# Encoder step on one core: the output product keeps six of its eight weight blocks between its last two column chunks, and the feed-forward layer's first operands are made while those chunks run

## The chip, the cores and the metric

The kernel runs on one core of a Trainium2 chip. The metric is the device time of one execution in microseconds (us); lower is better. Runs of the kernel before took 2792.56, 2794.83 and 2790.57 us (median 2792.56).

## The reference

One step of a two-layer encoder over 1024 prompt frames and 64 sample frames (1088 columns, 1024 features). Each layer adds a mixer (attention in layer 0; forgetting attention and a recurrent branch in layer 1) and a SwiGLU feed-forward network (FFN) to `x`, each behind an RMS norm. The change touches the end of the mixer, where its outputs are multiplied by `w_out` and added to `x`, and the start of the FFN:

```
o_a = (rmsnorm(o_a, a_subln_g) * (1.0 - lam_init)).reshape(nb, T, A_WIDTH)
o_b = o_b.reshape(nb, T, B_WIDTH)
return jnp.concatenate([o_a, o_b], axis=-1) @ w_out, new_state
...
yp = yp + mp
yp = yp + swiglu(rmsnorm(yp, norm_ffn_g[layer]), ffn_w1[layer], ffn_w3[layer], ffn_w2[layer])
...
def swiglu(h, w1, w3, w2):
    return (jax.nn.silu(h @ w1) * (h @ w3)) @ w2
```

The 64 sample frames go through the same products with the same weights.

## The kernel before

Every fp32 operand of a large product is cut into a high and a low part: `split` (L216) copies the high part on ScalarE (ACT, L217) and subtracts it from the operand on VectorE (DVE) or GpSimd (POOL, L218) for the low part. A product is then three matmuls on TensorE (PE): high·high, high·low, low·high. Features lie on 128 partitions in eight blocks; the 1088 columns are cut into three chunks of 384, 384 and 320.

**The output product.** `wout` (L822) runs chunk 0, then 1, then 2. In each chunk it takes the eight weight blocks of 128 output features two at a time, in the order 0, 2, 4, 6. `loadw` (L220) loads a block of 512 KB (128x1024) into one of two raw slots, `split` makes its high part on ACT and its low part on POOL, and these go into one of four slots that a ring hands out (`w_o`). So all eight blocks are loaded and split anew in every chunk: 24 loads a layer. After the last matmuls of a pair (L246 in `gemm_steps`), L848 on DVE adds the product in the PSUM banks to `x`, and `addsq` (L266) squares the result on ACT (L271 for a chunk's first block, L274 for the others) and adds it to the chunk's sum on DVE (L275). When a chunk's eight blocks are done, `rms` (L250) sums over partitions with a matmul of ones (L256), forms the inverse root by Ln (L260, L262) and Exp (L263) on ACT, and `norm_x` (L888) scales the eight blocks of `x` on DVE (L892).

**The first superblock of the FFN.** The two first FFN products are computed in a form with seven products of half-size blocks (`superblock`, L984): its PE instructions are L1000, each 128x272, 168 of them in a superblock. The right-hand operands T0 to T6 are sums and differences of normalised blocks of `x`, in high and low parts; `fill_x` (L899) makes them on ACT and DVE (L217, L218; the differences are L925), once for columns 0 to 543 (`p` = 0), once for columns 544 to 1087 (`p` = 1). The left-hand operands come from two weight blocks: `raws` (L961) loads them into two of three raw slots, and `left` (L940) makes four sums and differences of 128x512 on POOL (L953 to L956), seven high parts on ACT and seven low parts of 128x512 on the engine it is told. For superblock 0, `open_ffn` (L972) calls it ahead of the last pair of chunk 2 and has the low parts made on DVE; later superblocks have them on POOL. Superblock 0 runs `p` = 0 before `p` = 1, the later ones both together. L1004, L1008, L1010 (and L1061, L1062 with Silu) take the results from the banks.

**What sets the order.** The program is written as Python that emits instructions; a scheduler (the Tile framework) then puts them in an order for each engine, and inserts semaphores where data or a slot has to be waited for. Each engine runs its own list strictly in order. All loads and stores are issued by one queue, SP (L170). ACT loads a table of functions where the next function is not in the loaded one (`ACT_TABLE_LOAD`): Ln and Exp share one table, Silu is in another.

Of the kernel before, what the change touches and what calls it, by code (L numbers as in the profile page):

```python
# [58 lines left out]
F_RAW3 = (1024, 2048, 13440)  # L59
F_SUM = (14464, 14976)  # L60
F_C = (11776, 12320, 12864)
F_SG = (9600, 7424, 6144)
HB = 272
# [64 lines left out]
class Kernel:  # L128
    def __init__(self, tc, M, MR, PS, xTd, oTd, ed, fd, hd, I, O):
# [15 lines left out]
        self.w_o = at([0, 1024, R_Q[0], R_Q[0] + 1024]), at([2048, 3072, R_Q[0] + 2048, R_K[0]])  # L145
# [676 lines left out]
    def wout(self, W, gcol, src, l):  # L822
# [13 lines left out]
        def products(ms, ws, ci, ring):  # L836

            c0, n = CH[ci]
            for m in ms:
                self.dma(self.x[m][ci], src[m * 128:m * 128 + 128, c0:c0 + n])  # L840
            ps = [ring.get()[:, :n] for _ in ms]
            for p, w in zip(ps, ws):
                yield from self.gemm_steps(p, w, c0, n, oh, ol, ks[:-1], last=False)
            yield "w", 1
            for m, p, w in zip(ms, ps, ws):
                xs = self.x[m][ci]
                yield from self.gemm_steps(p, w, c0, n, oh, ol, ks[-1:], first=False)
                nc.vector.tensor_tensor(xs, p, xs, op=ALU.add)  # L848
                self.addsq(ci, m, xs)
                self.dma(self.xTd[m * 128:m * 128 + 128, c0:c0 + n], xs)  # L850

        load(0)
# [10 lines left out]
        fill = self.fill_x(0)  # L863
        ws = [self.loadw(W[i], self.w_o) for i in range(2)]
        for m in (0, 2, 4, 6):
            now = ws
            if m < 6:
                ws = [self.loadw(W[m + 2 + i], self.w_o) for i in range(2)]
            else:
                self.open_ffn(l)  # L870
            yield from products((m, m + 1), now, 2, self.mmf)
            if fill and m < 6:
                fill.pop(0)()
        self.tmp = self.tmp3
        r = self.rms(2)
        for f in fill:
            f()
        self.norm_x(2, gcol, r)
        for f in self.fill_x(1):
            f()  # L880
# [18 lines left out]
    def fill_x(self, p):  # L899
# [15 lines left out]
        def pieces(*hs):  # L915
            return [(0, HB)] if all(h == whole for h in hs) else list(zip(cuts, cuts[1:]))

        def put(i, f, h):
            for s, e in pieces(h):
# [3 lines left out]
        def sub(to, a, b):  # L923
            for s, e in pieces(to[1], a[1], b[1]):
# [3 lines left out]
        def mid():  # L928
            sub(b11, b12, b11)
            sub(b12, b22, b12)  # L930
            sub(b22, b22, b11)
            put(3, *b22)

        def end():
            sub(b21, b21, b22)
            put(6, *b21)
        return [lambda: put(0, *b11), lambda: put(1, *b21), lambda: put(2, *b22), mid,
                lambda: put(4, *b11), lambda: put(5, *b12), end]

    def left(self, a, b, adds, subs):  # L940

        a11, a12, a21, a22 = a[:, 0:512], a[:, 512:1024], b[:, 0:512], b[:, 512:1024]
        s1, s2 = (self.v(o, 512) for o in F_SUM)
# [10 lines left out]
        adds.tensor_tensor(s2, s1, a11, op=ALU.subtract)  # L954
        adds.tensor_tensor(a12, a12, s2, op=ALU.subtract)
        adds.tensor_tensor(a21, a11, a21, op=ALU.subtract)  # L956
        yield got
        for x in (a12, s2, s1, a21, a22):
            yield put(x)

    def raws(self, s):  # L961
# [3 lines left out]
        for j in (s - s % 2, s - s % 2 + 1):  # L965
            raw = self.v(F_RAW3[self.ri % 3], 1024)
# [5 lines left out]
    def open_ffn(self, l):  # L972
# [5 lines left out]
        r = self.raws(0)  # L978
        self.ops = list(self.left(*r, self.nc.gpsimd, self.nc.vector))
# [507 lines left out]
```

## Time and profile before

| | value |
|---|---|
| median of three runs | 2792.56 us (2790.57 to 2794.83) |
| the profiled execution: time, span | 2788.72 us, 2786.9 us |
| mean granted TensorE clock | 0.976 of full speed |
| busy share of the span: PE, DVE, ACT, POOL | 94%, 50%, 44%, 46% |
| loads of `w_out` blocks, both layers | 48 of 512 KB |
| layer 0: chunk 1's sum over partitions (L256), end of chunk 2's matmuls, chunk 2's L256, PE without a stop from | 645.04, 674.58, 690.25, 718.76 us |
| layer 1: the same | 1982.31, 2011.13, 2022.90, 2052.68 us |

The times of the last two rows are counted from the start of the span; a row of the timeline gives a start, a duration, the engine, the line, the operation with its operands, a count, and in brackets the idle time before it with what ended it. Neighbouring instructions of one shape are drawn together (x176), short gaps included. In the windows view the columns are the busy time of each engine inside a stretch.

### The profile page before, as it was taken

How to read it: one execution, taken by the hardware profiler on the slowest of the kernel's cores; microseconds unless marked ns; L12 is line 12 of the kernel's file. 1: busy time of each engine (PE TensorE's matmuls, PEld its weight loads, DVE VectorE, ACT ScalarE, POOL GpSimd, SP SyncE). 2: the span in 40 equal slices, each digit the busy share in tenths (PEclk: the TensorE clock that was granted, in tenths of full speed). 3: DMA queues.
4: the chain of work that ended last, by engine and by line, in shares of the span. 5: the costliest groups of instructions: out<-in, count | busy, mean ns of one | idle time of the engine just before them, and what ended most of it. 6: DMA issues, size and time to landing. Idle time of an engine off the chain costs nothing.

```text
span 2786.9 us, 45330 instructions
## 1 busy us (share of the span) xinstructions
PE 2615.1 (94%) x17614; PEld 2539.0 (91%) x17614; DVE 1405.8 (50%) x2753; ACT 1239.3 (44%) x2413; POOL 1284.4 (46%) x996
## 2 busy tenths in 40 slices
PE   6999999987899999999988789998889999999997
PEld 5899999987899999999978789988789999999997
DVE  7666666778532332422267547777962332342225
ACT  5666677754323323311245556676433323331113
POOL 5222222334766766312474333343566666741235
PEclk9999999998999999999999899999999999999998
DMA  6222222353222222532342342245422222244224
GB/s 197 69 70 73 69 62 63 114 170 116 78 102 70 79 78 78 192 102 70 108 139 36 47 88 79 76 124 163 129 83 90 86 78 70 79 157 143 70 65 143
DMA packets 122167, 272.11 MB, mean 98 GB/s; under 512 B 22216, under 2 KB 71632, under 8 KB 121952
## 3 DMA queue, kind: packets, MB, share of 16 engines
q1 hardware_dynamic: 121952, 269.22, 31.7%
q8 instruction: 138, 2.26, 0.3%
q14 instruction: 77, 0.63, 0.1%
HBM read 200.98 MB, written 65.43 MB: 96 GB/s over the span
## 4 chain that ended last, share of the span: by engine, by line
PE 71%; DVE 10%; ACT 6%; DMA 5%; POOL 3%; issue 3%; SPq 0%; DVEq 0%; ACTq 0%; POOLq 0%
PE banks L1000 31%; PE banks L246 13%; PE banks L1101 5%; PE banks L1102 5%; PE banks L1100 5%; DVE split_arena L218 3%; ACT split_arena L217 3%; PE banks L574 3%; POOL split_arena L218 2%; PE banks L457 2%; PE banks L458 1%; PE banks L499 1%; PE banks L500 1%; DVE arena L275 1%; DMA arena<-o_spill 1%
## 5 line engine op out<-in xcount | busy, mean ns | idle before, releaser
L218 POOL TENSOR_TENSOR split_arena<-arena,split_arena 128x512 fp32r<-128x512 f32 (+5 forms) x536 | 852.0, 1596 | 1129.6 <-ACT split_arena L217 1050.4
L217 ACT ACTIVATE split_arena<-arena 128x512 fp32r<-128x512 f32 (+10 forms) x713 | 506.7, 723 | 1130.3 <-PE banks L1000 439.2
L1000 PE MATMUL banks<-split_arena 128*128 128x272 f32 x7392 | 942.3, 290 | 39.8 <-ACT split_arena L217 16.1
L1000 PEld LDWEIGHTS banks<-split_arena 128*128 128x128 f32 x7392 | 937.8, 190 | 44.0 <-ACT split_arena L217 23.2
L246 PE MATMUL banks<-split_arena 128*128 128x384 f32 (+1 forms) x3528 | 666.4, 336 | 18.0 <-DVE arena L1264 7.1
L246 PEld LDWEIGHTS banks<-split_arena 128*128 128x128 f32 x3528 | 590.3, 192 | 28.1 <-DVE arena L1264 7.4
L1100 PE MATMUL banks<-split_arena 128*128 128x384 f32 (+1 forms) x1056 | 347.7, 329 | 4.7 <-DVE arena L1067 2.9
L1102 PE MATMUL banks<-split_arena 128*128 128x384 f32 (+1 forms) x1056 | 347.0, 329 | 2.4 <-POOL split_arena L218 2.4
L1101 PE MATMUL banks<-split_arena 128*128 128x384 f32 (+1 forms) x1056 | 346.4, 328 | 2.3 <-DVE split_arena L218 2.3
L218 DVE TENSOR_TENSOR split_arena<-arena,split_arena 128x1088 fp32r<-128x1088 f32 (+11 forms) x177 | 197.7, 1128 | 75.3 <-ACT split_arena L217 74.2
L218 DVE TENSOR_TENSOR split_arena<-banks,split_arena 128x512 fp32r<-128x512 f32 (+4 forms) x312 | 167.7, 542 | 97.4 <-ACT split_arena L217 94.7
L1100 PEld LDWEIGHTS banks<-split_arena 128*128 128x128 f32 x1056 | 200.0, 189 | 7.2 <-ACT split_arena L217 3.3
L1102 PEld LDWEIGHTS banks<-split_arena 128*128 128x128 f32 x1056 | 199.9, 189 | 3.3 <-POOL split_arena L218 3.1
L1101 PEld LDWEIGHTS banks<-split_arena 128*128 128x128 f32 x1056 | 200.1, 189 | 3.0 <-DVE split_arena L218 2.6
L469 DVE CUSTOM_DVE_ANT_0 arena<-banks,arena 128x384 f32<-128x384 f32 (+4 forms) x368 | 175.6, 494 | 47.1 <-PE banks L458 39.8
L217 ACT ACTIVATE split_arena<-banks 128x512 fp32r<-128x512 f32 (+4 forms) x312 | 146.8, 476 | 110.5 <-PE banks L574 46.1
L1008 DVE TENSOR_TENSOR arena<-banks,arena 128x544 f32<-128x544 f32 (+1 forms) x46 | 32.0, 699 | 295.4 <-PE banks L1000 295.4
L1121 DVE TENSOR_TENSOR arena<-banks,arena 128x384 f32<-128x384 f32 (+1 forms) x96 | 51.4, 535 | 251.7 <-PE banks L1102 251.5
L471 ACT ACTIVATE arena<-arena 128x640 f32<-128x640 f32 (+8 forms) x216 | 156.3, 724 | 42.8 <-DVE arena L469 41.3
L574 PE MATMUL banks<-arena 128*128 128x128 f32 (+2 forms) x828 | 133.3, 273 | 13.4 <-ACT arena L492 6.2
L574 PEld LDWEIGHTS banks<-arena 128*128 128x128 f32 (+2 forms) x828 | 95.4, 140 | 30.4 <-ACT arena L492 11.2
L457 PE MATMUL banks<-split_arena 128*128 128x256 f32 (+3 forms) x312 | 113.1, 364 | 6.4 <-DVE arena L469 4.3
(166 smaller groups left out, 3071.8 us busy)
## 6 DMA issues: line engine op xcount, KB each, us to landing
arena<-in_w_dram SPq DMA_DIRECT2D x120, 512.0 KB, 3.5
h_spill<-arena SPq DMA_DIRECT2D x22, 1088.0 KB, 4.3
arena<-h_spill SPq DMA_DIRECT2D x44, 544.0 KB, 4.7
arena<-in_w_dram SPq DMA_DIRECT2D x48, 384.0 KB, 3.2
arena<-in_abw_dram SPq DMA_DIRECT2D x24, 512.0 KB, 3.6
arena<-in_abo_dram SPq DMA_DIRECT2D x24, 512.0 KB, 3.7
arena<-in_cdo_dram SPq DMA_DIRECT2D x24, 512.0 KB, 3.6
arena<-in_cdw_dram SPq DMA_DIRECT2D x20, 512.0 KB, 3.7
```

Source lines behind the costliest of these rows:

```text
L217: self.nc.scalar.activation(hi, x, AF.Copy)
L218: return sub.tensor_tensor(lo, x, hi.bitcast(F32), op=ALU.subtract)
L246: self.pe = self.nc.tensor.matmul(ps, x[:, k], y[k][:, c0:c0 + n], start=a and i == 0, stop=z and i == 2).ins
L457: nc.tensor.matmul(ps[:, :mw], qd[:, q0:q0 + m], kk[:, k0 + s:k0 + s + mw], start=True, stop=False)
L469: nc.vector.tensor_tensor_reduce(o, p, t, -1.0, low, ALU.add, ALU.min, to)
L471: nc.scalar.activation(sb, sb, AF.Exp, bias=st[:, 0:1], scale=-1.0, accum_out=st[:, 1:2])
L574: nc.tensor.transpose(pt[:r, t * nq + s * m:t * nq + s * m + m], src, self.ident[:m, :m])
L1000: nc.tensor.matmul(bank[:, p], l[:, k], r[:, k, x], start=first and i == 0, stop=k == 3 and i == 2, skip_group_check=True)
L1100: nc.tensor.matmul(ps, wh, h[:, c0:c0 + n], start=j == j0, stop=False)
L1101: nc.tensor.matmul(ps, wh, lo[:, c0:c0 + n], start=False, stop=False)
L1102: nc.tensor.matmul(ps, wl, h[:, c0:c0 + n], start=False, stop=j == j1 - 1)
L1121: nc.vector.tensor_tensor(xs, ps, xs, op=ALU.add)
```

## The change

- The ring of four slots becomes six fixed pairs of slots (a pair holds the high and low parts of two blocks) a, b and c; c lies where the attention kept data that is dead by then. Chunk 0 takes the blocks as before through a and b. Then c is filled with blocks 0 and 1. Chunk 1 runs 6 (in b), 4 (in a), 0 (in c), 2 (loaded into b once 6 is done); chunk 2 runs 4, 0, 2 from the slots where they lie, and 6, loaded into a once 4 is done. A layer has 14 loads and splits of blocks instead of 24. The first block of a chunk, which starts the sum of squares, is now 0, 6 or 4.
- `open_ffn` is called after chunk 2's first pair instead of ahead of its last. There are four raw slots instead of three, the first of which (14464) is not shared with the raw weight slots, so that its load does not wait for them. Three of the steps of `left` are emitted after the pair 0, the others after the pair 2. The seven low parts of superblock 0 are made on POOL instead of DVE, and the sum that had a buffer of its own now takes the place of a block it used.
- `fill_x` is cut into finer steps. For `p` = 0, T0, T1 and parts of two differences come in chunk 1 and T2, T3 in chunk 2 (T2, which lies in c, once that is free); T4 to T6 come after chunk 2. For `p` = 1 only T0 and T1's first part (224 columns) is emitted ahead of chunk 2's end.

```diff
-        self.w_o = at([0, 1024, R_Q[0], R_Q[0] + 1024]), at([2048, 3072, R_Q[0] + 2048, R_K[0]])
+        self.w_o = (0, 1024, R_Q[0], R_Q[0] + 1024, R_Q[1], R_QL[0]), (2048, 3072, R_Q[0] + 2048, R_K[0], R_Q[1] + 1024, R_QL[0] + 1024)
...
-                self.addsq(ci, m, xs)
+                self.addsq(ci, m, xs, first=m == (0, 6, 4)[ci])
...
-        for m in (0, 2, 4, 6):
-            yield from products((m, m + 1), [self.loadw(W[m + i], self.w_o) for i in range(2)], 0, self.mma)
+        a, b, c = (tuple(zip(*(x[i:i + 2] for x in self.w_o))) for i in (0, 2, 4))
+        def weights(m, at):
+            return [self.loadw(W[m + i], [Ring(self.MR, [o], 1024) for o in at[i]]) for i in range(2)]
+        for m, at in ((0, a), (2, b), (4, a), (6, b)):
+            ws[m] = weights(m, at)
+            yield from products((m, m + 1), ws[m], 0, self.mma)
...
+        ws[0] = weights(0, c)
         self.norm_x(0, gcol)
-        for m in (0, 2, 4, 6):
-            yield from products((m, m + 1), [self.loadw(W[m + i], self.w_o) for i in range(2)], 1, self.mmf)
+        one, two = self.fill_x(0), self.fill_x(1)
+        for m in (6, 4, 0, 2):
+            yield from products((m, m + 1), ws[m], 1, self.mmf)
+            if m == 6:
+                ws[2] = weights(2, b)
+            else:
+                one.pop(0)()
         self.norm_x(1, gcol)
...
+        for m in (4, 0, 2, 6):
+            yield from products((m, m + 1), ws[m], 2, self.mmf)
+            if m == 4:
+                ws[6] = weights(6, a)
+                first = self.open_ffn(l)
+                one.pop(0)()
+            elif m == 0:
+                self.ops = [next(first) for _ in range(3)]
+                one.pop(0)()
+                two.pop(0)()
+            elif m == 2:
+                self.ops += list(first)
+                one.pop(0)()
...
-        self.ops = list(self.left(*r, self.nc.gpsimd, self.nc.vector))
+        return self.left(*self.raws(0), self.nc.gpsimd, self.nc.gpsimd)
```

Three places in the engines' own order matter later; all are from layer 0, and lines behind the change have shifted (L892 became L908, L925 L942, L953 to L956 L980 to L983, L1004 L1030, L1062 L1088).

ACT at the end of chunk 2, before: Ln and Exp of chunk 2's norm (L262, L263) stand together, ahead of the first Silu (L1062).

```order
L274 ACTIVATE arena<-arena 128x320 x2
L1004 ACTIVATE arena<-banks 128x272
L262 ACTIVATE arena<-banks,arena 128x320
L263 ACTIVATE arena<-arena 128x320
L1062 ACT_TABLE_LOAD
L1062 ACTIVATE arena<-banks 128x272
```

The same place of ACT after the change.

```order
L274 ACTIVATE arena<-arena 128x320 x2
L1030 ACTIVATE arena<-banks 128x272
L262 ACTIVATE arena<-banks,arena 128x320
L1088 ACT_TABLE_LOAD
L1088 ACTIVATE arena<-banks 128x272
L263 ACT_TABLE_LOAD
L263 ACTIVATE arena<-arena 128x320
```

A table load, the first Silu and a second table load now stand between Ln and Exp. In layer 1 they do not; there the order is as before.

POOL from chunk 0 to the first FFN operands, before: the x22 are the last splits of weight blocks of all three chunks, and the adds of `left` follow.

```order
L218 TENSOR_TENSOR split_arena<-arena,split_arena 128x1024 x22
L953 TENSOR_TENSOR arena<-arena 128x512
L954 TENSOR_TENSOR arena<-arena 128x512
L956 TENSOR_TENSOR arena<-arena 128x512
L955 TENSOR_TENSOR arena<-arena 128x512
```

The same place of POOL after the change; the two 128x512 in the second row are the first low parts of FFN operands, the x2 behind them blocks 6 and 7 for chunk 2.

```order
L218 TENSOR_TENSOR split_arena<-arena,split_arena 128x1024 x10
L218 TENSOR_TENSOR split_arena<-arena,split_arena 128x512 x2
L218 TENSOR_TENSOR split_arena<-arena,split_arena 128x1024 x2
L980 TENSOR_TENSOR arena<-arena 128x512
L981 TENSOR_TENSOR arena<-arena 128x512
L218 TENSOR_TENSOR split_arena<-arena,split_arena 128x512
L982 TENSOR_TENSOR arena<-arena 128x512
L218 TENSOR_TENSOR split_arena<-arena,split_arena 128x512
L983 TENSOR_TENSOR arena<-arena 128x512
L218 TENSOR_TENSOR split_arena<-arena,split_arena 128x512 x5
```

Ten splits of 128x1024 are gone, and superblock 0's low parts stand between and behind its adds; the last three of the x5 include two of superblock 0 and one of superblock 1.

DVE between the second pair of chunk 2 and the last, before: the 128x512 are the seven low parts of superblock 0.

```order
L848 TENSOR_TENSOR arena<-banks,arena 128x320 x2
L925 TENSOR_TENSOR arena<-arena 128x4x160
L275 TENSOR_TENSOR arena<-arena 128x320 x2
L218 TENSOR_TENSOR split_arena<-arena,split_arena 128x512 x2
L848 TENSOR_TENSOR arena<-banks,arena 128x320 x2
L218 TENSOR_TENSOR split_arena<-arena,split_arena 128x4x272
L275 TENSOR_TENSOR arena<-arena 128x320
L218 TENSOR_TENSOR split_arena<-arena,split_arena 128x512
L275 TENSOR_TENSOR arena<-arena 128x320
L218 TENSOR_TENSOR split_arena<-arena,split_arena 128x512 x4
L848 TENSOR_TENSOR arena<-banks,arena 128x320 x2
```

The same stretch of DVE after the change.

```order
L848 TENSOR_TENSOR arena<-banks,arena 128x320 x2
L942 TENSOR_TENSOR arena<-arena 128x4x112
L275 TENSOR_TENSOR arena<-arena 128x320
L942 TENSOR_TENSOR arena<-arena 128x4x160
L275 TENSOR_TENSOR arena<-arena 128x320
L942 TENSOR_TENSOR arena<-arena 128x4x112
L942 TENSOR_TENSOR arena<-arena 128x4x160
L848 TENSOR_TENSOR arena<-banks,arena 128x320 x2
L218 TENSOR_TENSOR split_arena<-arena,split_arena 128x4x112
L275 TENSOR_TENSOR arena<-arena 128x320
L218 TENSOR_TENSOR split_arena<-arena,split_arena 128x4x160
L275 TENSOR_TENSOR arena<-arena 128x320
```

No 128x512 is left, and pieces of the differences and of T3 (112 and 160 columns) stand in their place. On PE, chunk 2's L256 stands behind 28 matmuls of superblock 0 in each layer, where it stood behind 19 in layer 0 and 22 in layer 1.

More of the change, by code (lines that the diff above doesn't have):

```diff
@@ L858, in wout @@
         self.mm = self.mmf
+        ws[0] = weights(0, c)
         self.norm_x(0, gcol)
-        for m in (0, 2, 4, 6):
-            yield from products((m, m + 1), [self.loadw(W[m + i], self.w_o) for i in range(2)], 1, self.mmf)
-        self.norm_x(1, gcol)
[L863 to L873, printed above, removed]
+        one, two = self.fill_x(0), self.fill_x(1)
[5 more added lines that the diff above has]
+                one.pop(0)()
+        self.norm_x(1, gcol)
+        first = None
+        for m in (4, 0, 2, 6):
[11 more added lines that the diff above has]
+                one.pop(0)()
         self.tmp = self.tmp3
         r = self.rms(2)
-        for f in fill:
-            f()
+        one.pop(0)()
         self.norm_x(2, gcol, r)
-        for f in self.fill_x(1):
+        one.pop(0)()
+        for f in two:
             f()
@@ L913, in fill_x, with pieces, put, sub @@
         whole = 0 if p == 0 else 1
[L915 to L919, printed above, removed]
+        def pieces(hs, part):
+            p = [(0, HB)] if all(h == whole for h in hs) else list(zip(cuts, cuts[1:]))
+            return p if part is None else p[part:part + 1]
+        def put(i, f, h, part=None):
+            for s, e in pieces([h], part):
                 d = slice(HB * p + s, HB * p + e)
                 self.split(self.tgroup(i, 0)[:, :, d], self.tgroup(i, 1)[:, :, d], at(f, h, s, e), nc.vector)
[L923 to L924 removed]
+        def sub(to, a, b, part=None):
+            for s, e in pieces([to[1], a[1], b[1]], part):
                 nc.vector.tensor_tensor(at(*to, s, e), at(*a, s, e), at(*b, s, e), op=ALU.subtract)
         b11, b12, b21, b22 = (0, 0), (0, 1), (1, 0), (1, 1)
[L928 to L930 removed]
+        def t13(part=None):
+            sub(b11, b12, b11, part)
+            sub(b12, b22, b12, part)
+        def t2():
+            put(2, *b22)
             sub(b22, b22, b11)
[L932 to L934 removed]
+        def t4():
             sub(b21, b21, b22)
             put(6, *b21)
[L937 to L938 removed]
+        def steps(*fs):
+            return lambda: [f(*a) for f, *a in fs]
+        if p == 0:
+            return [steps((put, 0, *b11)), steps((put, 1, *b21)), steps((t13, 0)), steps((t13, 1)), steps((t2,)),
+                    steps((put, 3, *b22)), steps((put, 4, *b11), (put, 5, *b12)), steps((t4,))]
+        return [steps((put, 0, *b11, 0), (put, 1, *b21, 0)), steps((put, 0, *b11, 1), (put, 1, *b21, 1)),
+                steps((put, 2, *b22), (t13,), (sub, b22, b22, b11)), steps((put, 3, *b22)),
+                steps((put, 4, *b11), (put, 5, *b12)), steps((t4,))]
     def left(self, a, b, adds, subs):
         a11, a12, a21, a22 = a[:, 0:512], a[:, 512:1024], b[:, 0:512], b[:, 512:1024]
[L943 removed]
+        s1 = self.v(F_SUM, 512)
         def put(x):
```

14 lines of the change are left out of this document (7 added, 7 removed).

## The prediction

> **What bounds the kernel now.** The page comes first, then PE's timeline around the two places that the change touches.
>
> ```profile
> PE 2615.1 (94%) x17614; PEld 2539.0 (91%) x17614; DVE 1405.8 (50%) x2753; ACT 1239.3 (44%) x2413; POOL 1284.4 (46%) x996
> ```
>
> PE is busy 94% of 2786.9 us, so only its stops can be won: the change takes no matmul away. These are PE's rows in layer 0, from chunk 1's L256 on; a bracket is idle time with what ended it.
>
> ```profile
> 645.04 1.65 PE L256 MATMUL banks<-arena 128*128 128x384 f32 x2 [5.66 <-DVE arena L275]
> 645.92 28.66 PE L246 MATMUL banks<-split_arena 128*128 128x320 f32 x176
> 685.83 3.33 PE L1000 MATMUL banks<-split_arena 128*128 128x272 f32 x14 [11.26 <-ACT split_arena L217]
> ...
> 690.25 0.70 PE L256 MATMUL banks<-arena 128*128 128x320 f32 x2
> ...
> 718.76 61.47 PE L1000 MATMUL banks<-split_arena 128*128 128x272 f32 x473 [3.48 <-DVE arena L1008]
> ```
>
> And in layer 1.
>
> ```profile
> 1966.87 10.29 PE L246 MATMUL banks<-split_arena 128*128 128x384 f32 x60 [1.22 <-POOL split_arena L218]
> 1982.31 1.62 PE L256 MATMUL banks<-arena 128*128 128x384 f32 x2 [5.15 <-DVE arena L275]
> 1983.15 27.98 PE L246 MATMUL banks<-split_arena 128*128 128x320 f32 x178
> ...
> 2022.90 0.92 PE L256 MATMUL banks<-arena 128*128 128x320 f32 x2
> ...
> 2052.68 97.57 PE L1000 MATMUL banks<-split_arena 128*128 128x272 f32 x758 [3.48 <-DVE arena L1008]
> ```
>
> The brackets of these rows alone hold 20.4 us in layer 0 and 9.9 in layer 1. From 718.76 and 2052.68 on PE runs on without a stop, so whatever makes that moment earlier shortens the kernel, and nothing later in the FFN does.
>
> What sets that moment is seen in the windows view, from chunk 1's L256 to chunk 2's L256 and, in layer 0, from DVE's norm to the end of the stops. Its columns are the stretch, its length, then PE, PEld, DVE, ACT, POOL.
>
> ```profile
> 645.04:690.25 45.21, 33.59 (x197) 32.51 (x198) 35.85 (x41) 19.88 (x31) 21.30 (x10) 0.82 0.39 120
> 1982.31:2022.90 40.59, 33.27 (x202) 31.79 (x203) 36.22 (x42) 18.83 (x30) 19.06 (x9) 0.88 0.39 122
> 692.05:718.80 26.75, 17.05 (x118) 15.83 (x116) 26.75 (x26) 12.54 (x20) 18.27 (x11) 0.88 0.18 58
> ```
>
> After the norm starts, DVE has no idle time in layer 0 (26.75 of 26.75): DVE, not PE and not the weights, is the bound there. Ahead of it DVE is busy 35.85 of 45.21 us and 36.22 of 40.59. A stop that PE loses early comes back as a later one unless DVE gets there earlier too. DVE's own rows show how much of its time is not its own work.
>
> ```profile
> 653.90 0.81 DVE L925 TENSOR_TENSOR arena<-arena 128x640 f32<-128x640 f32 x1
> 657.26 3.03 DVE L925 TENSOR_TENSOR arena<-arena 128x640 f32<-128x640 f32 x1
> 674.62 1.29 DVE L218 TENSOR_TENSOR split_arena<-arena,split_arena 128x512 fp32r<-128x512 f32 x2 [3.89 <-ACT split_arena L217]
> ```
>
> The first two are one operation on one size, 2.22 us apart. These are POOL's at that time.
>
> ```profile
> 654.09 5.51 POOL L218 TENSOR_TENSOR split_arena<-arena,split_arena 128x1024 fp32r<-128x1024 f32 x2 [5.68 <-ACT split_arena L217]
> ...
> 708.79 9.34 POOL L218 TENSOR_TENSOR split_arena<-arena,split_arena 128x512 fp32r<-128x512 f32 x5 [0.74 <-ACT split_arena L217]
> ```
>
> The short one began ahead of POOL's splits; the long one lay beside them until 659.60: 2.34 us of overlap, 2.22 lost.
>
> **The change part by part.** The durations of the moved operations are in the groups of 645 to 719 us (count, then busy time and mean).
>
> ```profile
> L218 POOL TENSOR_TENSOR split_arena<-arena,split_arena 128x1024 fp32r<-128x1024 f32 x5 | 13.0, 2616 | 10.3 <-ACT split_arena L217 10.3
> L218 DVE TENSOR_TENSOR split_arena<-arena,split_arena 128x512 fp32r<-128x512 f32 x7 | 5.1, 778 | 4.6 <-ACT split_arena L217 4.6
> L218 POOL TENSOR_TENSOR split_arena<-arena,split_arena 128x512 fp32r<-128x512 f32 x7 | 12.8, 1855 | 0.7 <-ACT split_arena L217 0.7
> L218 DVE TENSOR_TENSOR split_arena<-arena,split_arena 128x448 fp32r<-128x448 f32 x1 | 0.6, 618 | 0.0
> ```
>
> *Chunk 1.* Six of its eight weight splits go. In these rows the sum of squares and the operand pieces that end chunk 1 stand beside them.
>
> ```profile
> 628.96 0.55 DVE L275 TENSOR_TENSOR arena<-arena 128x384 f32<-128x384 f32 x1
> ...
> 638.50 2.25 DVE L218 TENSOR_TENSOR split_arena<-arena,split_arena 128x448 fp32r<-128x448 f32 x1
> 641.93 3.05 DVE L275 TENSOR_TENSOR arena<-arena 128x384 f32<-128x384 f32 x2 [1.18 <-ACT arena L274]
> ```
>
> A 448 piece takes 0.618 us where POOL leaves it alone, so 1.6 are lost; the two L275 lose 1.9 against two of 0.55, and 1.2 is a wait for ACT, which was splitting a weight. Together 4.7 of the stop of 5.66. I leave 1.0 of each stop standing, because the first two low parts of FFN operands now run on POOL at chunk 1's end: 4.7 won in layer 0, 4.15 in layer 1, where the 1.22 us wait for a weight split goes too. Sum **10.1**; ends 6 (half the stretch stays) and 12.0 (all three stops go).
>
> *Chunk 2 up to its L256.* DVE loses the seven low parts (5.1 us busy) and takes three pieces over from chunk 1 (T2's 448 at 0.62, two differences of the same size, some 1.9 together). Its wait of 3.89 for the late operands goes in layer 0; layer 1 has 4.4 us idle in all, mostly the norm's, and I count 0.5 there. POOL has two weight splits instead of four or five (2.6 each) but seven low parts (1.855 each) and the adds: 5.2 + 13.0 + 4 × 1.6 = 24.6 us against 21.30 and 19.06. The 640 piece lost 2.22 us in 2.34 of overlap, a share of 0.95; but POOL is also busy while DVE reads PSUM or idles, so I take one half (ends 0 and 1): that adds 1.7 and 2.8. So layer 0: 5.1 − 1.9 + 3.9 − 1.7 = 5.4; layer 1: 5.1 − 1.9 + 0.5 − 2.8 = 0.9. Further down it can't go than PE allows: 28 matmuls stand ahead of L256, so some 6 us behind the end of chunk 2's, where it was 15.7 and 11.8 behind. PE's other inputs, POOL's chain: pair 4 releases its slots 7 us into chunk 2; ACT's split, POOL's (2.6), the raw block's landing and eight operations of 1.6 to 1.9 come to some 21 us, just at the end of chunk 2's matmuls. They are hidden, with 3 to 5 us to spare.
>
> *Ln and Exp.* These are ACT's rows of chunk 2's norm in layer 0.
>
> ```profile
> 690.99 0.53 ACT L262 ACTIVATE arena<-banks,arena 128x320 f32<-128x320 f32 x1 [1.52 <-PE banks L256]
> 691.55 0.47 ACT L263 ACTIVATE arena<-arena 128x320 f32<-128x320 f32 x1
> 692.04 1.28 ACT L1062 ACT_TABLE_LOAD   x1
> 693.33 0.40 ACT L1062 ACTIVATE arena<-banks 128x272 f32<-128x272 f32 x1
> ```
>
> Now two loads and a Silu come between the first two: 1.28 + 0.40 + 1.28 = 3.0 us during which the scaling on DVE, and behind it every operand of `p` = 1, waits. A third load, for the next Silu, is hidden behind the splits. I take **−3.0** in layer 0, none in layer 1; what hides some of it is DVE's L1034 ahead of the scaling, at most 0.4. The Trainium skill (ScalarE: Activation LUTs, What ACT_TABLE_LOAD costs) gives about 2.7 us with the drain for a load; by that it would be an estimated 5.8 us here, but the Silu's start 1.29 us after the load's shows none of the extra.
>
> *From the norm on.* The scaling and the sixteen operations for `p` = 1 are the same; POOL's load is the same in kind (superblock 1's operands), so the block keeps its length: **0**, ends 0 and 8 (first rival). The 20 loads of 512 KB that go were on no stop that the rows name besides those counted; the fourth raw slot changes nothing where PE doesn't wait.
>
> Sum: 10.1 + (5.4 − 3.0) + 0.9 = 13.4. PE's granted clock, 0.82 to 0.90 in the three windows, should rise as its stops shrink; its work there lies under DVE's bound, so I give that 1 to 2. Together **15**. The profiled execution took 2788.72, 3.8 under the median of the runs; against that median the forecast is **2777.5**.
>
> **The rivals.**
>
> *More is won (2764).* The adds of superblock 1 no longer wait for a raw slot, since there are four. In layer 0 the second waited for its load until DVE was amid `p` = 1, which began with T0's low part.
>
> ```profile
> 695.76 0.35 DVE L218 TENSOR_TENSOR split_arena<-arena,split_arena 128x192 fp32r<-128x192 f32 x1
> ...
> 699.63 1.36 POOL L954 TENSOR_TENSOR arena<-arena 128x512 f32<-128x512 f32 x1 [10.75 <-DMA arena<-in_w_dram]
> ```
>
> If three adds run during the scaling, the block of 23.0 us (695.76 to 718.76) loses three stretches of some 1.3 (0.95 of 1.36): 3.9 a layer; and with chunk 2's L256 at PE's own bound, 3 more in each. 2777.5 − 13.8 = 2764. For: the 10.75 us wait for the load. Against: the low parts of superblock 1 wait for slots that superblock 0's `p` = 1 releases, and stay. Chance 0.20.
>
> *POOL takes back what DVE was spared (2782.5).* If the two engines exclude each other while both read operands from SBUF, then a microsecond of POOL costs DVE one: the extra 3.3 and 5.5 us count whole and the gain of chunk 2 is 5.1 − 1.9 + 3.9 − 3.3 − 3.0 = 0.8 and −1.8. Only chunk 1's 10.1 is left: 2782.5. The 2.22 us by which the 640 piece grew in 2.34 us speak for it. Against it: DVE's L848 reads PSUM, and up to L256 DVE idles 9.4 of 45.21 us, where a stretch costs nothing. The Trainium skill says just this (SBUF — State Buffer, Who interferes with whom): the port pair shared by DVE and GpSimd is an exclusive lock, for which a DVE instruction with two SBUF inputs contends; by that rule the trace agrees. Chance 0.17.
>
> *Slower (2796).* The left operands are still late. Chunk 2's L256 now stands behind 28 matmuls, and these need POOL's eighth operation behind the raw block's landing (in layer 1 the tenth). If that block lands only as late as before, when the first add began at 675.49, 0.9 us behind the last matmul, the eighth ends 15 us and the tenth 19 us behind it. In layer 0 DVE's row ahead of the scaling (L1034, a product that needs the tenth) then holds it until 22 us behind that end, where it began 17.5 behind (692.05): +4.5. In layer 1 L256 comes 21 behind for 11.8: +9. Less 10.1, that is +3.5. It decides once the first add starts later than the end of chunk 2's matmuls. For: SP's loads stand behind eight stores that wait for L848. Against: a raw slot that shares nothing, and a call a whole chunk earlier. Chance 0.08.
>
> ```profile
> 675.49 1.55 POOL L953 TENSOR_TENSOR arena<-arena 128x512 f32<-128x512 f32 x1 [8.23 <-DMA arena<-in_w_dram]
> ```
>
> That the change isn't made is excluded by the lists: 14 loads a layer for 24.
>
> **How the numbers follow.** Forecast 0.55, the rivals 0.20, 0.17 and 0.08. Its own ends are 2772 (chunk 1 at 12, L256 at PE's bound in one layer) and 2784 (chunk 1 at 6, stretch whole in layer 1). The range 2757 to 2788 takes in the first rival with 7 us for its unknown length and the second; outside lie the third and the rest of the first, under 2 in 10. A change under 0.2% (5.6 us) is about what a measurement of this kernel can't tell from none: faster by more needs under 2787, which leaves out the third rival and the lower ends of the second: 0.83; within 0.2%: 0.10; slower: 0.07.
>
> **What would show it.** Right: chunk 1's L256 with a stop of about 1 us in both layers; no 128x512 on DVE in chunk 2; the stop behind chunk 2's matmuls down from 11.26 to 2 to 4; L256 37 to 39 us behind chunk 2's start; in layer 0 Exp 3 us behind Ln's end; 23 us from T0's low part to the run without stops. Wrong: that stretch under 20 us (first rival), DVE busy without a pause from chunk 2's start to L256 with its L218 and L942 at two or three times their shortest rows (second), or PE's first matmuls of superblock 0 waiting for POOL (third).

## The result and the profile after

| | before | after |
|---|---|---|
| median of four runs | 2793.59 us | 2765.97 us (2762.25 to 2769.05) |
| the profiled execution: time, span | 2788.72, 2786.9 us | 2767.11, 2765.3 us |
| mean granted clock of that execution | 0.976 | 0.979 |

The ratio is 0.9901, with a 95% interval of 0.9889 to 0.9914: the change takes 27.6 us off, where 15 were forecast. The two profiled executions lie closer together, 21.6 us, since that of before was 4.9 us under the median of its runs and that of after 1.1 over. The steps below are weighed against these 21.6.

PE's rows after the change, from chunk 0's sum over partitions in layer 0 to the run without stops (L1026 is the former L1000).

```profile
614.03 1.65 PE L256 MATMUL banks<-arena 128*128 128x384 f32 x2 [5.34 <-DVE arena L275]
641.63 0.91 PE L256 MATMUL banks<-arena 128*128 128x384 f32 x2
642.09 26.27 PE L246 MATMUL banks<-split_arena 128*128 128x320 f32 x176
...
674.57 0.60 PE L1026 MATMUL banks<-split_arena 128*128 128x272 f32 x1 [6.09 <-DVE split_arena L218]
...
680.31 0.70 PE L256 MATMUL banks<-arena 128*128 128x320 f32 x2
...
711.26 68.99 PE L1026 MATMUL banks<-split_arena 128*128 128x272 f32 x542 [0.33 <-DVE arena L1087]
```

And in layer 1.

```profile
1932.36 0.91 PE L256 MATMUL banks<-arena 128*128 128x384 f32 x2
...
1965.21 0.91 PE L256 MATMUL banks<-arena 128*128 128x384 f32 x2
1965.66 26.26 PE L246 MATMUL banks<-split_arena 128*128 128x320 f32 x176
...
2002.39 1.00 PE L256 MATMUL banks<-arena 128*128 128x320 f32 x2
...
2030.15 120.12 PE L1026 MATMUL banks<-split_arena 128*128 128x272 f32 x942 [1.19 <-DVE arena L1034]
```

Chunk 1's L256 waits for nothing now (5.66 and 5.15 before), and the stop behind chunk 2's matmuls is 6.09 where it was 11.26. Two rows of the kernel before, chunk 0's L256 in each layer, complete the marks.

```profile
613.92 0.91 PE L256 MATMUL banks<-arena 128*128 128x384 f32 x2 [1.70 <-DVE arena L275]
...
1943.53 0.91 PE L256 MATMUL banks<-arena 128*128 128x384 f32 x2
```

| stretch between two L256 | before | after | difference | forecast |
|---|---|---|---|---|
| start to layer 0's chunk 0 | 613.92 | 614.03 | +0.1 | 0 |
| layer 0, chunk 0 to 1 | 31.12 | 27.60 | -3.5 | -4.7 |
| layer 0, chunk 1 to 2 | 45.21 | 38.68 | -6.5 | -5.4 |
| layer 0's chunk 2 to layer 1's chunk 0 | 1253.28 | 1252.05 | -1.2 | +3.0 |
| layer 1, chunk 0 to 1 | 38.78 | 32.85 | -5.9 | -5.4 |
| layer 1, chunk 1 to 2 | 40.59 | 37.18 | -3.4 | -0.9 |
| layer 1's chunk 2 to the end | 764.00 | 762.91 | -1.1 | 0 |

The forecast's remaining 1.6 us were for the clock and had no place of their own. The fourth row says little about the change: it holds the whole mixer of layer 1, and from layer 1's first L256 to its chunk 0's alone two profiles of the changed kernel have 544.50 and 549.46 us. What bears on the change is the part up to the start of the last of superblock 0's 168 matmuls. From chunk 2's L256 to there it took 33.33 us in layer 0 and takes 33.36 (forecast: 3.0 more); in layer 1 it took 34.90 and takes 32.33 (forecast: the same).

The windows view of the two stretches of chunk 2 after the change, for the rows of before in the prediction; the granted clock is the last column but two.

```profile
641.63:680.31 38.68, 32.39 (x207) 31.51 (x207) 35.89 (x38) 16.84 (x28) 22.72 (x12) 0.91 0.28 89
1965.21:2002.39 37.18, 32.93 (x207) 32.11 (x207) 35.06 (x38) 16.87 (x28) 21.88 (x12) 0.92 0.30 93
```

DVE is busy for 35.89 and 35.06 us, where it was for 35.85 and 36.22. What shrank is its idle time, from 9.4 to 2.8 us and from 4.4 to 2.1. The granted clock rose from 0.82 and 0.88. DVE's timeline in chunk 2 and behind it, layer 0 of the changed kernel:

```profile
654.37 7.77 DVE L218 TENSOR_TENSOR split_arena<-arena,split_arena 128x896 fp32r<-128x896 f32 x4
...
694.29 2.36 DVE L942 TENSOR_TENSOR arena<-arena 128x896 f32<-128x896 f32 x3
...
699.23 1.10 DVE L218 TENSOR_TENSOR split_arena<-arena,split_arena 128x896 fp32r<-128x896 f32 x1
709.20 0.96 DVE L218 TENSOR_TENSOR split_arena<-arena,split_arena 128x192 fp32r<-128x192 f32 x1 [8.88 <-ACT split_arena L217]
```

POOL's over the same time:

```profile
657.67 2.14 POOL L218 TENSOR_TENSOR split_arena<-arena,split_arena 128x512 fp32r<-128x512 f32 x1
...
693.10 8.36 POOL L218 TENSOR_TENSOR split_arena<-arena,split_arena 128x512 fp32r<-128x512 f32 x1 [21.74 <-ACT split_arena L217]
```

And ACT's, from chunk 2's Ln (L262) to its Exp (L263) and on:

```profile
681.05 0.53 ACT L262 ACTIVATE arena<-banks,arena 128x320 f32<-128x320 f32 x1 [2.16 <-PE banks L256]
681.60 1.28 ACT L1088 ACT_TABLE_LOAD   x1
682.89 0.40 ACT L1088 ACTIVATE arena<-banks 128x272 f32<-128x272 f32 x1
683.30 1.28 ACT L263 ACT_TABLE_LOAD   x1
684.60 0.47 ACT L263 ACTIVATE arena<-arena 128x320 f32<-128x320 f32 x1
...
706.73 2.96 ACT L217 ACTIVATE split_arena<-arena 128x512 fp32r<-128x512 f32 x6 [8.90 <-POOL arena L983]
```

Four things stand in these rows. The two table loads and the Silu do stand between Ln and Exp, 3.0 us from 681.60 to 684.60. Behind the scaling, DVE's operand steps run at their shortest (three of 896 and 192 columns in 2.36 us) until 700.3. Meanwhile one low part of 128x512 takes POOL 8.36 us, where another took 2.14. And then DVE waits 8.88 us for ACT, which has waited 8.90 for POOL's last add (L983): on ACT the last piece of T6 stands behind four high parts of superblock 1's left operands. So the 22.5 us from T0's low part (688.81) to 711.26 are as long as the 23.0 before, for another reason.

### The profile page after: what moved, and what is told of

Its sections match the earlier page's. It is cut to its first block, busy times and chain, and to the rows that moved or that the text cites. A ratio compares the mean times of both kernels' runs of the same rounds, so it can differ in the third digit from the quotient of the medians.

```text
span 2765.3 us, 45216 instructions
## 1 busy us (share of the span) xinstructions
PE 2613.0 (94%) x17614; PEld 2536.4 (92%) x17614; DVE 1367.8 (49%) x2739; ACT 1222.7 (44%) x2395; POOL 1253.5 (45%) x990
## 4 chain that ended last, share of the span: by engine, by line
PE 76%; DVE 8%; ACT 6%; DMA 4%; POOL 3%; issue 3%; SPq 0%; DVEq 0%; ACTq 0%; POOLq 0%
PE banks L1026 32%; PE banks L246 16%; PE banks L1127 6%; PE banks L1128 6%; PE banks L1126 6%; PE banks L574 3%; ACT split_arena L217 2%; DVE split_arena L218 2%; POOL split_arena L218 2%; PE banks L457 2%; PE banks L458 1%; PE banks L499 1%; PE banks L500 1%; DMA arena<-o_spill 1%; DVE arena L275 1%
## 5 line engine op out<-in xcount | busy, mean ns | idle before, releaser
L218 POOL TENSOR_TENSOR split_arena<-arena,split_arena 128x512 fp32r<-128x512 f32 (+5 forms) x530 | 824.5, 1559 | 1176.0 <-ACT split_arena L217 1099.4
L217 ACT ACTIVATE split_arena<-arena 128x512 fp32r<-128x512 f32 (+10 forms) x693 | 486.6, 714 | 1111.8 <-PE banks L1026 441.0
L1026 PE MATMUL banks<-split_arena 128*128 128x272 f32 x7392 | 946.3, 291 | 29.0 <-DVE split_arena L218 13.3
L1026 PEld LDWEIGHTS banks<-split_arena 128*128 128x128 f32 x7392 | 941.1, 190 | 34.2 <-DVE split_arena L218 14.8
L218 DVE TENSOR_TENSOR split_arena<-arena,split_arena 128x1088 fp32r<-128x1088 f32 (+8 forms) x163 | 163.4, 1013 | 76.8 <-ACT split_arena L217 75.9
L574 PEld LDWEIGHTS banks<-arena 128*128 128x128 f32 (+2 forms) x828 | 95.9, 140 | 31.5 <-DVE arena L490 10.5
```

Of the source, the lines that this page charges most:

```text
L217: self.nc.scalar.activation(hi, x, AF.Copy)
L218: return sub.tensor_tensor(lo, x, hi.bitcast(F32), op=ALU.subtract)
L574: nc.tensor.transpose(pt[:r, t * nq + s * m:t * nq + s * m + m], src, self.ident[:m, :m])
L1026: nc.tensor.matmul(bank[:, p], l[:, k], r[:, k, x], start=first and i == 0, stop=k == 3 and i == 2, skip_group_check=True)
```

## The experiments

In the short diffs `A` is the changed kernel and `B` the kernel before. Each run was timed beside the kernel before on its own chip, and the ratios are to that.

**The slots alone**: `B` with the loops over `a`, `b`, `c` of the change (three places, each for the high and low parts of two blocks).

```diff
+        for m in (4, 0, 2, 6):
+            if m == 6:
+                self.open_ffn(l)
+            yield from products((m, m + 1), ws[m], 2, self.mmf)
+            if m == 4:
+                ws[6] = weights(6, a)
+            if m != 6:
+                fill.pop(0)()
```

> Only the weight slots of the change (14 loads a layer), the operands of superblock 0 made as before, with their low parts on DVE and the last two operand steps behind chunk 2. Theory (what delays chunk 1's end is POOL's weight splits beside DVE): chunk 1's L256 loses its stops, about 9 us over both layers as after the change (3.4 + 5.9), and two POOL splits fewer lie in chunk 2, worth 1 to 3: about 10 to 12 us under before, 2782 to 2784. Rival (the gain of chunk 1 comes back as a later wait, since the operands of superblock 0 are as late as before): the stop behind chunk 2's matmuls grows by what chunk 1 won, and the time stays at 2790 to 2794.

Measured: 2772.82 us, ratio 0.9916 (0.9903 to 0.9928), 21.1 us under before. These are PE's rows.

```profile
641.03 0.91 PE L256 MATMUL banks<-arena 128*128 128x384 f32 x2
...
678.91 0.70 PE L256 MATMUL banks<-arena 128*128 128x320 f32 x2
...
1970.46 0.91 PE L256 MATMUL banks<-arena 128*128 128x384 f32 x2
...
2006.42 0.70 PE L256 MATMUL banks<-arena 128*128 128x320 f32 x2
```

Chunk 1's stops are gone with the slots alone, and chunk 2's stretch is 37.88 and 35.96 us, shorter than in the whole change (38.68, 37.18), although the low parts are still on DVE. The rival (the gain comes back) fell. The theory was right on chunk 1 (9.3 us) and too small on chunk 2, which gave 12.0 instead of 1 to 3. There the left operands are ready sooner, since fewer weight splits hold the raw slots: POOL's first add for them starts 15.3 us behind chunk 1's L256, where before it started 30.5 us behind it (675.49).

```profile
656.34 1.92 POOL L960 TENSOR_TENSOR arena<-arena 128x512 f32<-128x512 f32 x1 [3.60 <-DMA arena<-in_w_dram]
```

**The operand half alone**, twice: `A` with the ring and the 24 loads of `B`, blocks 0, 2, 4, 6 in each chunk. In the first of the two the `elif` branch also makes T3; in the second T3 is made behind chunk 2.

```diff
+            if m == 0:
+                first = self.open_ffn(l)
+                one.pop(0)()
...
+            elif m == 4:
+                self.ops += list(first)
```

> The other half alone: 24 loads through the ring of four slots, blocks in the order 0, 2, 4, 6, but superblock 0's operands made early, its seven low parts on POOL, four raw slots, the finer operand steps. Theory: the two halves nearly add, so this one gives the chunk 2 part, 8 to 12 us less four more POOL splits beside DVE in chunk 2 (2.2 us of DVE each, half of it hidden, 4 a layer): 2786 to 2792. Rival (the operand half carries most of the 27.6 us): 2775 to 2780. Rival (POOL has no room for the low parts while it splits all weights): slower than before, 2797.

Measured: 2800.33 us, ratio 1.0023 (1.0014 to 1.0032). T3 lies in two slots of the ring, so that it was written over blocks that the last pair had yet to read, and the pair waited for it, as PE's timeline has it (layer 0; in layer 1 the stop is 11.65 us).

```profile
681.83 9.33 PE L246 MATMUL banks<-split_arena 128*128 128x320 f32 x46 [8.79 <-DVE split_arena L218]
```

These stops are the overlap's and not the operand half's, so the run says only that the early operands need a place that the ring has.

> The operand half alone, put right: 24 loads through the ring, blocks 0, 2, 4, 6, superblock 0's operands early with their low parts on POOL, but T3 (whose place the ring's last blocks use) made behind chunk 2. Theory after the first runs (POOL's splits beside DVE are the cost; this half takes none of them away and adds thirteen us of low parts): chunk 1 as before, chunk 2 no shorter, 2791 to 2797. Rival (the halves add, and the operand half brings what the slots alone lacked, 3 to 6 us): 2787 to 2790.

Measured: 2792.65 us, ratio 0.9995 (0.9986 to 1.0004). Here a block of `w_out` was loaded over FFN weights in a raw slot that both use, so the values of superblock 0 are other ones; the instructions are those meant. Its time can't be told from before: as far as this run shows, the early operands win nothing where the splits of 24 blocks stay, and they need raw slots that the loads of `w_out` don't use. The shared slot can have added waits of its own. On PE the stop ahead of chunk 1's L256 stands as before (5.52 us in layer 0), and the last pair of chunk 2 waits for POOL's splits.

```profile
678.88 8.84 PE L246 MATMUL banks<-split_arena 128*128 128x320 f32 x46 [4.69 <-POOL split_arena L218]
```

**The low parts back on DVE.**

```diff
-        return self.left(*self.raws(0), self.nc.gpsimd, self.nc.gpsimd)
+        return self.left(*self.raws(0), self.nc.gpsimd, self.nc.vector)
```

> The changed kernel with superblock 0's seven low parts back on DVE. Theory of the forecast (DVE is lengthened by half of POOL's busy time): DVE gets 5.1 us a layer, is freed of half of 13.0 = 6.5, so within 2 us of the changed kernel: 2764 to 2768. If POOL costs DVE its whole time: 8 a layer faster, 2750 to 2755. If POOL's low parts cost DVE little (they lie beside L848, L908 and idle time): 4 to 5 a layer slower, 2774 to 2777.

Measured: 2766.60 us, ratio 0.9896 (0.9883 to 0.9910). The whole time lies within the interval of the changed kernel, as the theory had it. PE's marks say more.

```profile
641.89 0.91 PE L256 MATMUL banks<-arena 128*128 128x384 f32 x2
...
678.10 0.70 PE L256 MATMUL banks<-arena 128*128 128x320 f32 x2
...
1966.32 0.91 PE L256 MATMUL banks<-arena 128*128 128x384 f32 x2
...
2000.72 0.81 PE L256 MATMUL banks<-arena 128*128 128x320 f32 x2
```

With the low parts back on DVE, chunk 2's stretch is 36.21 and 34.40 us, for 38.68 and 37.18. On POOL they thus cost 2.5 and 2.8 us more than on DVE: about 0.6 of the 13.0 us that the forecast gave POOL for them is felt (5.1 and some 2.6), where it had one half. Whether the whole time gains as much, the intervals can't tell.

**POOL's low parts of chunk 1 left out of the kernel before.**

```diff
-            yield from products((m, m + 1), [self.loadw(W[m + i], self.w_o) for i in range(2)], 1, self.mmf)
+            yield from products((m, m + 1), [self.loadw(W[m + i], self.w_o, low=False) for i in range(2)], 1, self.mmf)
```

> The kernel before, leaving out POOL's low parts of the eight weight blocks of chunk 1 (the products there read what the slots held); loads and ACT's high parts stay. Theory (POOL beside DVE is what delays chunk 1's end): the stops ahead of chunk 1's L256 (5.66 and 5.15 us) fall to under 2, and from chunk 0's L256 to chunk 1's it takes about 28 and 33 us, as after the change, instead of 31.1 and 38.8: 2782 to 2786 in all if it is kept. Rival (it is ACT's splits or the loads that DVE's L275 waits for): the stops stay above 4 and the time is within 2 us of before.

Measured: 2776.29 us, ratio 0.9935 (0.9923 to 0.9948): 17.6 us, with all loads and all of ACT's work still there. POOL's low parts cost these, then, and not the loads. But the stops ahead of chunk 1's L256 stayed, as the rival had it (4.11 us in layer 0, 3.96 in layer 1). These are layer 0's rows: PE's, then DVE's, then POOL's (this kernel's L259 and L278 are L256 and L275 of the others).

```profile
607.52 1.37 PE L259 MATMUL banks<-arena 128*128 128x384 f32 x2 [2.62 <-DVE arena L278]
638.17 1.30 PE L259 MATMUL banks<-arena 128*128 128x384 f32 x2 [4.11 <-DVE arena L278]
```

```profile
632.77 5.34 DVE L278 TENSOR_TENSOR arena<-arena 128x384 f32<-128x384 f32 x2
```

```profile
632.26 5.44 POOL L218 TENSOR_TENSOR split_arena<-arena,split_arena 128x1024 fp32r<-128x1024 f32 x2 [2.80 <-ACT split_arena L217]
```

The scheduler had drawn chunk 2's splits ahead into the empty place: two of them (5.44 us) lie beside the two sums of squares (L278) that end chunk 1, which take 5.34 instead of 1.1. Much of the gain was made earlier: chunk 0's L256 came at 607.52 instead of 613.92. In the kernel before, splits of chunk 1's blocks stood there beside low parts that DVE makes at the end of the attention.

```profile
599.60 4.97 POOL L218 TENSOR_TENSOR split_arena<-arena,split_arena 128x1024 fp32r<-128x1024 f32 x2 [10.04 <-ACT split_arena L217]
```

```profile
600.87 4.06 DVE L218 TENSOR_TENSOR split_arena<-arena,split_arena 128x320 fp32r<-128x320 f32 x2 [0.83 <-ACT split_arena L217]
```

In this run POOL does nothing at that place, and two of the same size take DVE 0.89 us.

```profile
605.02 0.89 DVE L218 TENSOR_TENSOR split_arena<-arena,split_arena 128x320 fp32r<-128x320 f32 x2 [1.54 <-ACT split_arena L217]
```

So POOL's splits cost at the end of the attention too, which neither theory had.

**The changed kernel again**, for a second profile.

> The changed kernel once more, for a second profile. If POOL's 8.36 us low part in layer 0 (all of it beside an undisturbed DVE) is fixed by the order of the two engines' starts, it is there again, with a stop of 6 to 7 us ahead of the run without stops; if it is chance, POOL's low parts there take 1.3 to 1.9 us and DVE's sixteen operations take 20 to 22 us instead of 12. Time 2762 to 2769 in both.

Measured: 2771.90 us, ratio 0.9912 (0.9897 to 0.9926). The time is a little above the 2762 to 2769 that were expected; the kernel before took 2795.63 beside it. POOL's timeline has the long low part again, so it wasn't chance of one execution.

```profile
694.62 8.54 POOL L218 TENSOR_TENSOR split_arena<-arena,split_arena 128x512 fp32r<-128x512 f32 x1 [21.84 <-DVE split_arena L218]
```

**Exp behind Ln.**

```diff
-                nc.scalar.activation(o, ps if add is None else o, AF.Silu)
+                with self.tc.issue_after(self.rexp.ins):
+                    nc.scalar.activation(o, ps if add is None else o, AF.Silu)
```

`rexp` is the Exp of the last norm; `issue_after` queues an instruction behind another on its engine.

> The changed kernel with Silu's steps queued behind Exp on ACT, so that in layer 0 no table load comes between Ln and Exp. Theory (the two loads and the Silu delay the scaling, 3.0 us, and the operands of p = 1 with it): 2 to 3 us under the changed kernel, 2763. Rival (what ends layer 0's stops is ACT's queue behind POOL's adds, so the delay is hidden): within 1 us of it, 2766.

Measured: 2773.10 us, ratio 0.9914 (0.9900 to 0.9927), beside 0.9912 of the changed kernel on the same chip. The intervals alone would leave room for 3 us; the profiles of the two leave none. Chunk 2's L256 in layer 0, here:

```profile
682.06 0.70 PE L256 MATMUL banks<-arena 128*128 128x320 f32 x2
```

And in the second profile of the changed kernel:

```profile
682.00 0.70 PE L256 MATMUL banks<-arena 128*128 128x320 f32 x2
```

The last of superblock 0's matmuls starts at 715.59 us here and at 715.62 there. The rival's time holds, its reason only in part: the scaling comes 3 us earlier, but in this run's profile POOL's long low part is gone, and DVE's steps beside POOL are long again instead, so that the same moment is reached in another way.

**Superblock 1's left operands behind the operand steps.**

```diff
+        self.filled = self.hi
...
+                    if s == 0:
+                        with self.tc.issue_after(self.filled.ins):
+                            got.append(next(nxt))
```

`hi` is ACT's last high part, here that of T6.

> The changed kernel with ACT's high parts of superblock 1's left operands queued behind its last operand step for superblock 0. Theory (two costs are left: in layer 0 the last piece of T6 stands on ACT behind four of these, which wait for POOL; in layer 1 POOL's ten operations lengthen DVE's sixteen from 12 to 22 us): 6 us in layer 0 and up to 8 in layer 1, 2752 to 2758. Rival (superblock 1's left operands are then late and PE waits there instead): within 2 us of the changed kernel or slower, 2764 to 2772.

Measured: 2759.40 us, ratio 0.9871 (0.9859 to 0.9884), 12.5 us under the changed kernel on the same chip. The rival fell; the theory's upper end is missed by 1.4 us.

**The two orders together**, this edit and Exp behind Ln.

> The two orders together. Theory: the gains add, 2750 to 2756, since Exp is now on the path in layer 0. Rival: as the better of the two alone.

Measured: 2757.08 us, ratio 0.9864 (0.9851 to 0.9876). That lies between the theory and the rival, and the further 2.3 us lie inside the intervals of the two. The profiles have them, though, where Exp comes earlier: from chunk 2's L256 to superblock 0's last matmul layer 0 takes 24.33 us, for 26.64 with the last edit alone. DVE's rows of this run, layer 0: the first and the last of the sixteen operations for `p` = 1.

```profile
682.63 0.35 DVE L218 TENSOR_TENSOR split_arena<-arena,split_arena 128x192 fp32r<-128x192 f32 x1
...
695.24 1.35 DVE L218 TENSOR_TENSOR split_arena<-arena,split_arena 128x896 fp32r<-128x896 f32 x2
```

POOL's at that time:

```profile
696.31 2.65 POOL L218 TENSOR_TENSOR split_arena<-arena,split_arena 128x512 fp32r<-128x512 f32 x2 [6.16 <-ACT split_arena L217]
```

From T0's low part to the end of T6's it takes 14.0 us (682.63 to 696.59), where the changed kernel took 21.4 (688.81 to 710.16). POOL's low parts start at 696.31, as DVE ends.

**The same order on the kernel before.**

> The kernel before with ACT's high parts of superblock 1's left operands queued behind the last operand step of superblock 0, and nothing of the change. Theory (the 23.0 us from T0's low part to the run without stops are POOL's operations for superblock 1 beside DVE's sixteen, whatever went ahead): the stretch falls to about 14 us and the time by 7 to 9 us in each layer less what PE then waits for the left operands, as from the changed kernel to its version with this order (12.5): 2780 to 2784. Rival (the wait for late left operands eats it): 2789 to 2794.

Measured: 2782.17 us, ratio 0.9960 (0.9947 to 0.9973), 12.3 us. The theory holds, and it is the same sum as on the changed kernel. From chunk 2's L256 to superblock 0's last matmul it takes 27.39 and 26.61 us, for 33.33 and 34.90. What POOL takes from DVE in the first superblock is separate from what the change does.

**The splits for the third pair of slots behind chunk 0's norm**, on top of both orders.

```diff
-        ws[0] = weights(0, c)
         self.norm_x(0, gcol)
+        x0 = self.rexp.ins
...
             if m == 6:
+                with self.tc.issue_after(x0):
+                    ws[0] = weights(0, c)
                 ws[2] = weights(2, b)
```

> Both orders on the changed kernel, and the load and splits of blocks 0 and 1 into the third pair of slots queued behind chunk 0's Exp instead of ahead of its last sums. Theory (the two splits of 4.97 us beside DVE's last L275 make the stop of 5.3 us ahead of chunk 0's L256 in layer 0): that stop falls to about 1, 3 to 4 us under the version with both orders: 2753 to 2755. Rival (the splits then fall beside DVE's operand steps of chunk 1 and its stop comes back there): 2756 to 2759.

Measured: 2739.14 us, ratio 0.9808 (0.9795 to 0.9821): 55.4 us under before, twice the change. The rival fell, and the theory was too small by 14 us. PE's marks in both layers:

```profile
604.68 0.91 PE L256 MATMUL banks<-arena 128*128 128x384 f32 x2 [0.31 <-DVE arena L275]
632.18 0.91 PE L256 MATMUL banks<-arena 128*128 128x384 f32 x2
...
1907.10 0.81 PE L256 MATMUL banks<-arena 128*128 128x384 f32 x2
```

DVE's L275 that the first of them waits for, here:

```profile
604.07 0.56 DVE L275 TENSOR_TENSOR arena<-arena 128x384 f32<-128x384 f32 x1
```

And in the version with both orders, beside the two splits:

```profile
606.32 5.49 DVE L275 TENSOR_TENSOR arena<-arena 128x384 f32<-128x384 f32 x3 [0.35 <-ACT arena L274]
```

The stop ahead of chunk 0's L256 is 0.31 us, where it was 5.22 in the version with both orders. The splits still meet DVE, now in its scaling, whose eight steps take 8.61 us instead of 4.32; but PE has chunk 1's matmuls to run meanwhile and doesn't stop.

```profile
607.48 8.61 DVE L911 SCALAR_TENSOR_TENSOR arena<-arena 128x384 f32<-128x384 f32 x8 [0.61 <-ACT arena L263]
```

Layer 1 gains more: its chunk 0's L256 comes 19.4 us earlier than in the version with both orders (1926.54 there), of which 6.7 come from layer 0 (611.40 there). Of the other 12.7, some 3.8 are seen in the rows of that version. Its two splits stand beside two low parts of 320 columns (0.89 us elsewhere) at the end of layer 1's attention, and behind these PE stops for 3.40 us.

```profile
1912.71 4.92 POOL L218 TENSOR_TENSOR split_arena<-arena,split_arena 128x1024 fp32r<-128x1024 f32 x2 [26.33 <-PE banks L457]
```

```profile
1913.30 4.69 DVE L218 TENSOR_TENSOR split_arena<-arena,split_arena 128x320 fp32r<-128x320 f32 x2
```

The rest lies mostly in layer 1's mixer, in which two profiles of one kernel differed by 5.0 us; what of it the splits cost, no run here separates.

## Why the prediction was right, and where it wasn't

**Right: who bounds these stages, and the stop of chunk 1.** DVE, held up by POOL, sets when PE may go on. Chunk 1 was to give 10.1 and gave 9.4 us; of its stops, of which 1.0 each was to stay, nothing stayed. That POOL's splits cost so much beside DVE's sums is shown by the last run: two of them taken away from chunk 0's sums bring its stop from 5.22 to 0.31 us. For chunk 1 itself it is read from rows: in the run that leaves its low parts out other splits take their place beside the same two sums, and the stop stays.

**Mis-sized: the term for chunk 2.** 6.3 us were forecast and 9.9 came. Two steps of its sum were wrong. "DVE loses the seven low parts (5.1 us busy)" was to leave DVE 1.5 and 0.4 us less to do, after what it takes over and what POOL adds; it has 0.0 and 1.2 less. POOL takes back what moved to it, and the slots alone give 12.0 in these stretches with the low parts still on DVE. What paid was DVE's waiting: 6.6 and 2.3 us of it went, where 3.9 and 0.5 were counted. For layer 1 the forecast had called its 4.4 us of idle time mostly the norm's. DVE's row of the kernel before shows it otherwise: it waited 3.18 us for late left operands, and 0.55 more at 2011.47.

```profile
2008.06 2.07 DVE L218 TENSOR_TENSOR split_arena<-arena,split_arena 128x512 fp32r<-128x512 f32 x2 [3.18 <-ACT split_arena L217]
```

These waits are gone with the slots alone, where the weight splits in chunk 2 fall from four or five to two and the left operands come sooner. No run has one of the two without the other. The stop behind chunk 2's matmuls was to fall to 2 to 4 us and fell to 6.09 only: the same 176 matmuls take 26.27 us instead of 28.66, but DVE runs without a pause from 643.76 us to 0.7 us ahead of L256, so that PE, done sooner, waits for DVE behind them. In this stretch the forecast's "under DVE's bound" is right; its windows show clocks of 0.82 to 0.88, not to 0.90.

**Mis-sized: the 3.0 us for the table loads.** They are in the trace, to a tenth as worked out (1.28 + 0.40 + 1.28), and they cost nothing here: from L256 to superblock 0's last matmul layer 0 takes 33.36 us for 33.33, and with Exp ahead of them that matmul comes at the same moment. They were hidden, not free. The forecast named what could hide them on DVE (at most 0.4) and didn't look at ACT's list behind them, where the last piece of T6 stands behind four high parts that wait for POOL's adds. Once these four stand elsewhere, Exp ahead of the loads wins 2.3 us of that stretch. By the Trainium skill (ScalarE: Activation LUTs, What ACT_TABLE_LOAD costs) two loads with their drains would be an estimated 5.3 us. The two took 2.56, and the instruction behind each started 1.29 and 1.30 us after the load's start, so that no drain shows.

**"The block keeps its length": right in its number only.** 22.5 and 21.9 us for 23.0. In layer 1 (2008.21 to 2030.15) it is DVE beside POOL as before; the 2.6 us won there up to superblock 0's last matmul are 1.0 in the scaling, 1.1 in the block and the rest behind it. In layer 0 DVE was done with all but the last piece by 700.3 and waited for ACT; and behind the mark PE has 14 matmuls of superblock 0 left where it had 24, which with the shorter stretch makes up the 3.0 us. The first rival gave a time near the measured one (2764 for 2765.97), but that is luck: the adds of superblock 1 didn't run during the scaling (in layer 0 they stood behind POOL's long low part, from 701.42 on), and L256 comes 12.0 and 10.5 us behind chunk 2's matmuls, not 6.

**Second rival: the rule holds, its price didn't follow.** Operations of two SBUF inputs on DVE and POOL do exclude one another in these runs (5.44 us of POOL, 5.34 of two L275 that take 0.55 each). By the Trainium skill (SBUF — State Buffer, Who interferes with whom) that is one lock for the pair, and the trace agrees. Its sign came too: DVE without a pause in chunk 2, and four splits in a row in 7.77 us (the row from 654.37 on), which take 3.35 with the slots alone. But it charged all of POOL's added time and left only chunk 1's gain; about 0.6 of POOL's time was felt when the low parts moved, and like the forecast it counted the waits that went at 3.9 and 0.5.

**The rest, some 6 us,** is between the medians and the profiled pair. The runs of the kernel before show mean clocks of 0.969 to 0.975 beside 0.976 in its profiled execution; that the spread is the clock's is argued from that, not shown. The slots alone took 21.1 us off, the whole change 27.6 and, timed again, 23.7, with intervals that overlap, so what the operand half adds on top of the slots stays open in the whole time. In the profiles it adds nothing: from chunk 0's L256 to superblock 0's last matmul the two layers together take 223.9 us before, 200.4 with the slots alone, 202.0 and 203.8 in the two profiles of the changed kernel, and 195.5 with the low parts back on DVE.

## What to carry to other kernels

Where DVE bounds a stage, count what POOL does beside it as DVE's time before counting DVE's own: moving work from DVE to POOL bought nothing here, and taking work from POOL, or moving it to where PE doesn't wait for DVE, bought 12 to 18 us each time. Split a bounding engine's stretch into busy and idle time, and name what ends each wait, before saying which will shrink. Read each engine's list behind a delay for the next wait before charging the delay. And of a change with two halves, run each: one carried nearly all of it, and on top of the two orders moving two of its splits a layer elsewhere was worth some 17 us more.

## What the runs showed of the hardware that was not expected

POOL's operation can be the one held, and for long: with nothing between DVE's operations, a 128x512 subtraction that takes 1.27 to 2.14 us elsewhere in layer 0 took 8.36 (693.10 to 701.46), over nine DVE operations at their shortest, and ended about 1.1 us after the last. It did so in both profiles of the changed kernel and not in layer 1 of either, where DVE and POOL take turns and many DVE operations are longer by about one of POOL's (2.37 us at 2013.33 for 1.29). What decides between the two, no run here tells.
